# Values of the memory for two heads at once and the Fourier input product in one: 512 moving columns

## The chip, the core and the metric

The kernel runs on one core of a Trainium2 chip. The metric is the device time of one execution in microseconds. Three runs of the kernel before took 1768.17, 1768.70 and 1770.47 us; the median is 1768.7. A profile comes from one more execution.

A core has several engines, each with its own queue of instructions, which it works off strictly in the order in which they stand: TensorE (PE) multiplies matrices, VectorE (DVE) and ScalarE (ACT) work on elements, SyncE (SP) issues the transfers from device memory (DMA), GpSimd (POOL) does next to nothing here. A matmul keeps a 128x128 block stationary in the array and streams the moving operand through it, up to 512 columns; sums gather in accumulators (`acc`), of which the mixing stage has four, each two banks of 512 columns wide.

## The reference, cut to what matters

An encoder of two layers works on two groups of tokens, 512 and 256, with 1024 channels. The even layer mixes by a depthwise convolution of 31 taps (half the channels) and by a Fourier transform along the tokens and inside groups of 128 channels (the other half); the odd layer mixes by average pools of four widths. Each layer then attends with four heads of 256 channels to 256 memory tokens per group, and ends in a gated feed-forward block.

```python
def trunk(...):
    for l in range(DEPTH):
        h = rms_norm(x, norm_mix[l])
        if l % 2 == 0:
            u = h @ w_in_even[e]
            a = conformer_conv(u[..., :D_CONV], u[..., D_CONV:2 * D_CONV], ...)
            f = fourier_mix(u[..., 2 * D_CONV:])
            x = x + jnp.concatenate([a, f], axis=-1) @ w_out_even[e]
        else:
            x = x + multiscale_pool(h, w_pool[o], pool_scale[o])
        x = x + memory_cross_attn(rms_norm(x, norm_xa[l]), rms_norm(mem, norm_mem[l]), ...)
        x = x + swiglu(rms_norm(x, norm_ffn[l]), ...)
...
    kv = (mem_n @ wkv).reshape(b_, m_, 2, XA_HEADS, XA_HEAD_DIM)
    k, v = kv[:, :, 0], kv[:, :, 1]
```

Two products matter here: `u[..., 1024:]`, the Fourier input (768 tokens, 1024 channels in, 512 out), and `v`, the values of the memory (512 memory tokens of both groups, 1024 channels in, 256 out for each head, in both layers).

## The kernel before

**Split numbers.** Every float32 operand of a product is split into an upper and a lower part of a shorter type. `split` (L147, L148) makes the upper part by a copy on ACT (`wh`) and the lower one by a subtraction on DVE (`wl`). A product is the sum of three matmuls, upper x upper, upper x lower, lower x upper, so a block of weights can be used in full only when DVE has made its lower part.

**Weights.** `unit` fetches 128x1024 numbers of weights (512 KB) into one of four buffers `raw` and splits them into two of seven buffers `w`. A buffer is free again when the matmuls that read it are done.

**Even mixer.** `mixer_even` first makes the convolution's two input halves. Each finished chunk of 128 channels adds a generator of taps to a list (`taps`, 46 instructions of 128x392 on DVE at L433 for each of four chunks, each adding to the result of an earlier one); `pump(n)` issues n of them between other work. Then come the Fourier input (`uf`), with the normalized tokens stationary and the weights moving; the transform, four times `along_sequence` and `across_channels`; what is left of keys and values; the sum of the four convolution chunks (`total`, L584 to L586); and the output projection (`project`, `center`).

**Keys and values.** `keys_values` is a generator, which `advance(kv)` moves on by one `yield`. For each head it makes the keys (two units, 24 matmuls of 512 columns each) and the values: both units of weights are fetched and split, and then for each of four blocks of 128 memory tokens 24 matmuls of 256 columns run over the eight blocks of channels into a quarter of one accumulator; when all four are done ACT evicts them (L402). It yields four times for each head. The even mixer advances it once before the transform, twice in it, 12 times in the loop with `pump(8)`, once behind `total`. The odd mixer (`mixer_odd`) advances it twice at its start, once for each of eight pools, and then to the end; behind it come the splits of x for the attention (`split_x`, L150 on ACT, L151 on DVE) and the query product.

**Fourier input.** In two halves of 256 output channels; in each, the token blocks go three to an accumulator, each with 24 matmuls over the eight blocks of channels. ACT and DVE evict the three (L513, L514: a copy and a subtraction, which are the upper and lower part) behind the last of them, with four taps behind each.

**What sets the order.** The program is written as loops, but a scheduler reorders the instructions of each engine by estimated costs and fixes their order when the kernel is built. On the chip nothing moves. It also places the waits: a matmul that writes to an accumulator waits for what reads that accumulator, if that stands ahead of it in the program, whichever of the two banks it reads.

Of the kernel before, what the change touches and what calls it, by code (L numbers as in the profile page):

```python
# [11 lines left out]
F32R = mybir.dt.float32r  # L12
I32 = mybir.dt.int32
AF = mybir.ActivationFunctionType
ALU = mybir.AluOpType
# [50 lines left out]
def trunk_kernel(ctx, tc, x_in, m_in, mt_in, vec_in, cst_in, win, wf, wout, wpool, wq, wk, wv, wo, wgu, wd, out):  # L66
# [35 lines left out]
    def nm(s):  # L102
        cnt[0] += 1
        return f"{s}_{cnt[0]}"
# [25 lines left out]
    def big():  # L130

        return acc.tile([P, 512 * banks], F32, tag="acc", name=nm("acc"))
# [8 lines left out]
    def asf(ap):  # L141
        return ap.bitcast(F32)

    def split(hi, lo, src, gain=None):

        if gain is None:
            nc.scalar.activation(hi, src, AF.Copy)  # L147
            nc.vector.tensor_tensor(lo, src, asf(hi), ALU.subtract)  # L148
        else:
            nc.scalar.activation(hi, src, AF.Copy, scale=gain)  # L150
            nc.vector.scalar_tensor_tensor(lo, src, gain, asf(hi), ALU.mult, ALU.subtract)  # L151
# [26 lines left out]
    def unit(src, n=1024):  # L178

        return parts(fetch(src, n), n)  # L180

    def mm(o, a, b, start, stop, more=False):
        nc.tensor.matmul(o, a, b, start=start, stop=stop, skip_group_check=more)  # L183

    def prod(outs, w, xs, start, stop, more=False):

        wh, wl = w
        for o, (xh, xl) in zip(outs, xs):
            mm(o, wh, xh, start, False, more)
        for o, (xh, xl) in zip(outs, xs):  # L190
            mm(o, wh, xl, False, False, more)
        for o, (xh, xl) in zip(outs, xs):
            mm(o, wl, xh, False, stop, more)

    def cut(p, s):
        return p[0][:, s], p[1][:, s]
# [173 lines left out]
    def keys_values(l, ms, ks, vs):  # L370


        room = stream(512, F32)
        for h in range(HEADS):

            r = [next(room) for _ in range(4)]
            ks.extend([r[0], r[3]])
            ps = big()
            for f in range(2):
                w = unit(wk[l, h * 2 + f])  # L380
                for k in range(KD):
                    prod([ps[:, f * 512 : f * 512 + 512]], cut(w, slice(k * P, (k + 1) * P)), [ms[k]], k == 0, k == KD - 1)
                if f == 0:
                    yield
            for f in range(2):
                nc.scalar.activation(ks[h * 2 + f], ps[:, f * 512 : f * 512 + 512], AF.Copy)
            yield
            w = [unit(wv[l, h, j]) for j in range(2)]
            for r_ in r[1:3]:
                vs.extend([r_[:, :256], r_[:, 256:]])  # L390
            ps = big()
            for t in range(4):
                o = ps[:, t * 256 : (t + 1) * 256]
                for k in range(KD):
                    m_, w_ = cut(ms[k], slice(t * P, (t + 1) * P)), cut(w[k // 4], slice((k % 4) * 256, (k % 4 + 1) * 256))
                    mm(o, m_[0], w_[0], k == 0, False)
                    mm(o, m_[0], w_[1], False, False)
                    mm(o, m_[1], w_[0], False, k == KD - 1)
                if t == 1:
                    yield  # L400
            for t in range(4):
                nc.scalar.activation(vs[h * 4 + t], ps[:, t * 256 : (t + 1) * 256], AF.Copy, scale=mem["r"][:, t : t + 1])  # L402
            yield


    def mixer_even(l, e, first):
# [77 lines left out]
            gated(i, *p)  # L484

        uf = list(zip(blocks(NB, 512), blocks(NB, 512)))
        for j in range(2):
            w = [unit(wf[e, j, 0])]
            if j == 0:
                w.append(unit(wf[e, j, 1]))  # L490
            w = [[cut(u, slice(i * 256, (i + 1) * 256)) for i in range(4)] for u in w]
            if j == 1:
                raw = fetch(wf[e, j, 1])
                hi = wp.tile([P, 1024], F32R, tag="w", name=nm("wh"))
                w.append([])
                for i in range(2):
                    lo, a = hp.tile([P, 512], F32R, tag="h", name=nm("h")), i * 512
                    split(hi[:, a : a + 512], lo, raw[:, a : a + 512])
                    w[1].extend((hi[:, a + b : a + b + 256], lo[:, b : b + 256]) for b in (0, 256))
            for b2 in range(2):  # L500
                ps = big()
                for bb in range(3):
                    b = b2 * 3 + bb
                    o = ps[:, bb * 256 : (bb + 1) * 256]
                    for k in range(KD):
                        x_, w_ = cut(hs[k], slice(b * P, (b + 1) * P)), w[k // 4][k % 4]
                        mm(o, x_[0], w_[0], k == 0, False)
                        mm(o, x_[0], w_[1], False, False)
                        mm(o, x_[1], w_[0], False, k == KD - 1)
                for bb in range(3):  # L510
                    b = b2 * 3 + bb
                    o, u_ = ps[:, bb * 256 : (bb + 1) * 256], cut(uf[b], slice(j * 256, (j + 1) * 256))
                    nc.scalar.activation(u_[0], o, AF.Copy, scale=rt[:, b : b + 1])  # L513
                    nc.vector.scalar_tensor_tensor(u_[1], o, rt[:, b : b + 1], asf(u_[0]), ALU.mult, ALU.subtract)  # L514
                    pump(4)
                if j == 0 and b2 == 0 and "R" not in mem:
                    mem["R"] = stay(token_row(mem["r"], TM), TM, cst, "Rm")

        F = []
        dft = list(zip(blocks(6, 512), blocks(6, 512)))  # L520
# [86 lines left out]
                split(p[0], p[1], xc[i])  # L607
                ln["A"].append(p)

        for _ in range(12):  # L610
            advance(kv)
            pump(8)
        tot = total()
        advance(kv, 1)
        project(1, F, (0,))
# [635 lines left out]
def _arrange(i):  # L1251
    C = np.ascontiguousarray
    k8 = lambda w: w.reshape(KD, P, -1, P).transpose(2, 1, 0, 3)
    d = {}
    d["x"] = _chunks(np.concatenate([i["x_prompt"][0], i["x_sample"][0]], axis=0))
    d["m"] = _chunks(np.concatenate([i["mem_prompt"][0], i["mem_sample"][0]], axis=0))
    d["mt"] = C(np.concatenate([i["mem_prompt"][0], i["mem_sample"][0]], axis=0)).reshape(-1, P, D)
    d["vec"] = C(np.concatenate([
        _cols(i["norm_mix"]), _cols(i["norm_xa"]), _cols(i["norm_mem"]), _cols(i["norm_ffn"]),
        _cols(i["norm_final"][None]), _cols(i["conv_b"]), _cols(i["conv_ln_g"]), _cols(i["conv_ln_b"]),  # L1260
        _cols(i["pool_scale"]),
        i["conv_w"][0].reshape(CW, NC, P).transpose(2, 1, 0).reshape(P, NC * CW),
    ], axis=1))
    d["cst"] = _constants()
    w = i["w_in_even"]
    val = [k8(a[:, :512]) for a in w]
    gate = [k8(a[:, 512:1024]) for a in w]
    d["win"] = C(np.stack([np.stack([g, a], axis=1) for g, a in zip(gate, val)])).reshape(-1, 8, P, 1024)
    d["wf"] = C(w[:, :, 1024:].reshape(-1, 2, 4, P, 2, 256).transpose(0, 4, 1, 3, 2, 5)).reshape(-1, 2, 2, P, 1024)
    d["wout"] = C(i["w_out_even"].reshape(-1, 2, 4, P, 4, 256).transpose(0, 1, 4, 3, 2, 5)).reshape(-1, 2, 4, P, 1024)  # L1270
    d["wpool"] = C(i["w_pool"].reshape(-1, 2, 2, 2, P, 256).transpose(0, 1, 4, 2, 3, 5)).reshape(-1, 2, P, 1024)
    d["wq"] = C(np.stack([k8(a) for a in i["xa_wq"]])).reshape(DEPTH, 8, P, 1024)
    d["wk"] = C(np.stack([k8(a[:, :D]) for a in i["xa_wkv"]])).reshape(DEPTH, 8, P, 1024)
    d["wv"] = C(i["xa_wkv"][:, :, D:].reshape(DEPTH, 2, 4, P, HEADS, 256).transpose(0, 4, 1, 3, 2, 5)).reshape(DEPTH, HEADS, 2, P, 1024)
    d["wo"] = C(i["xa_wo"].reshape(DEPTH, HEADS, 2, P, 2, 512).transpose(0, 1, 4, 3, 2, 5)).reshape(DEPTH, HEADS, 2, P, 1024)
    g = i["ffn_w_gate_up"].reshape(DEPTH, KD, P, 2, NF, P)
    d["wgu"] = C(g.transpose(0, 4, 3, 2, 1, 5)).reshape(DEPTH, NF, 2, P, 1024)
    wd = i["ffn_w_down"].reshape(DEPTH, NPAIR, 2, P, KD // 2, 2, P)
    rows = []
    for l in range(DEPTH):  # L1280

        parts = [wd[l, list(g)].transpose(3, 2, 4, 1, 0, 5).reshape(-1) for g in GROUPS[l]]

        slow = [q for q in range(NPAIR) if not any(q in g for g in GROUPS[l])]
        parts.append(wd[l, slow].transpose(3, 4, 2, 0, 1, 5).reshape(-1))
        rows.append(np.concatenate(parts))
    d["wd"] = C(np.stack(rows))
    return d
# [17 lines left out]
```

## Time and profile before

| | |
|---|---|
| median of three runs | 1768.7 us |
| the profiled execution | 1767.83 us |
| its span, from the first to the last instruction | 1765.7 us |
| TensorE busy | 1745.6 us, 99% |
| DVE busy | 1405.5 us, 80% |
| ACT busy | 762.8 us, 43% |
| matmuls of 128x256 from `wh`, `wl` and `h` | 704 + 328 + 24 |
| mean granted clock of TensorE | 0.997 |

Busy time is counted once where records overlap; a matmul's length is its whole latency, so the step from one start to the next is what it costs TensorE. In rows of the timeline the first number is the start, the second the length, both in us, and `x` the count. In groups the numbers behind the bar are busy time in us, mean length of one in ns, and idle time of the engine just before them with what ended it. Names such as `acc<-wh,s` read result, moving operand, stationary operand.

### The profile page before, as it was taken

Reading aid. Unit: us, or ns where it says so; the run is one execution under the profiler, and the core shown is the slowest. Engines: PE = TensorE matmul, PEld = TensorE weight load, DVE = VectorE, ACT = ScalarE, POOL = GpSimd, SP = SyncE. Lnnn points to the kernel's source line nnn. Section 1 sums busy time; section 2 is a strip of 40 time slices with the busy share of each in tenths; the row PEclk is TensorE's granted clock in tenths of the full one; section 3 lists DMA queues with packets and bytes.
Section 4 is the critical chain, followed back from the end, with each engine's and each line's share of the span. In section 5 each row is a group of like instructions: output and inputs, shape, how many; then the busy total and the mean of one; then the engine's idle time right before and its main releaser. Section 6 shows DMA issues by size and latency. Waiting matters only on the chain.

```text
span 1765.7 us, 26406 instructions
## 1 busy us (share of the span) xinstructions
PE 1745.6 (99%) x10362; PEld 1708.1 (97%) x10362; DVE 1405.5 (80%) x2327; ACT 762.8 (43%) x1287; POOL 2.5 (0%) x40
## 2 busy tenths in 40 slices
PE   9999999999999999999999999999999999999997
PEld 9999999999999999999999999999999999999996
DVE  7998976477788978788769984486888888879876
ACT  7233244253435555454336243352445555543331
POOL 0000000000000000000000000000000000000000
PEclk9999999999999999999999999999999999999998
DMA  7232221202214535456664332111215454547731
GB/s 255 84 108 61 92 77 48 60 22 63 60 48 173 197 135 197 137 181 247 250 234 131 95 96 63 46 48 48 60 36 189 151 189 143 197 171 273 267 86 72
DMA packets 60460, 224.74 MB, mean 127 GB/s; under 512 B 6704, under 2 KB 7984, under 8 KB 60336
## 3 DMA queue, kind: packets, MB, share of 16 engines
q1 hardware_dynamic: 60336, 223.06, 37.4%
q8 instruction: 81, 1.33, 0.3%
q14 instruction: 43, 0.35, 0.1%
HBM read 172.70 MB, written 50.33 MB: 126 GB/s over the span
## 4 chain that ended last, share of the span: by engine, by line
PE 93%; DVE 5%; DMA 1%; ACT 0%; issue 0%; SPq 0%; DVEq 0%; ACTq 0%
PE acc L183 92%; DVE s L151 1%; DVE c L279 1%; DVE s L148 1%; DVE x L323 1%; DVE s L1176 0%; DVE w L148 0%; DMA x<-in_x 0%; PE acc L751 0%; DVE x L816 0%; DMA raw<-in_wd 0%; DVE st L733 0%; DVE c L742 0%; DMA raw<-in_m 0%; DVE kl L148 0%
## 5 line engine op out<-in xcount | busy, mean ns | idle before, releaser
L183 PE MATMUL acc<-s,w 128*128 128x384 f32 x4800 | 835.4, 335 | 0.5 <-DVE x L816 0.4
L183 PEld LDWEIGHTS acc<-s,w 128*128 128x128 f32 x4800 | 831.8, 188 | 2.7 <-issue 0.8
L183 PE MATMUL acc<-s,wh 128*128 128x384 f32 (+2 forms) x2272 | 514.5, 342 | 5.7 <-DVE x L323 2.6
L183 PEld LDWEIGHTS acc<-s,wh 128*128 128x128 f32 x2272 | 403.3, 188 | 20.2 <-ACT Rx L268 3.0
L183 PE MATMUL acc<-s,wl 128*128 128x384 f32 (+2 forms) x1136 | 307.5, 341 | 0.0
L147 ACT ACTIVATE w<-raw 128x512 fp32r<-128x512 f32 (+1 forms) x304 | 181.5, 601 | 255.6 <-PE acc L183 236.0
L148 DVE TENSOR_TENSOR w<-raw,w 128x512 fp32r<-128x512 f32 (+1 forms) x304 | 196.0, 653 | 43.6 <-ACT w L147 39.7
L147 ACT ACTIVATE wh<-raw 128x1024 fp32r<-128x1024 f32 (+2 forms) x107 | 107.3, 1010 | 269.6 <-PE acc L183 252.2
L183 PEld LDWEIGHTS acc<-s,wl 128*128 128x128 f32 x1136 | 206.3, 188 | 5.3
L148 DVE TENSOR_TENSOR wl<-raw,wh 128x1024 fp32r<-128x1024 f32 (+2 forms) x105 | 122.4, 1173 | 77.7 <-PE acc L183 64.2
L183 PE MATMUL acc<-wh,s 128*128 128x256 f32 x704 | 129.0, 284 | 0.0
L816 DVE TENSOR_TENSOR x<-acc,x 128x384 f32<-128x384 f32 x168 | 92.6, 554 | 24.9 <-PE acc L183 24.2
L183 PEld LDWEIGHTS acc<-wh,s 128*128 128x128 f32 x704 | 110.7, 192 | 0.2
L323 DVE TENSOR_TENSOR x<-acc,x 128x768 f32<-128x768 f32 x80 | 76.2, 955 | 30.1 <-PE acc L183 30.0
L147 ACT ACTIVATE w<-sum 128x512 fp32r<-128x512 f32 (+1 forms) x120 | 71.9, 599 | 60.5 <-PE acc L183 42.5
L148 DVE TENSOR_TENSOR w<-sum,w 128x512 fp32r<-128x512 f32 (+1 forms) x120 | 78.4, 653 | 24.0 <-ACT w L147 23.5
L183 PE MATMUL acc<-wl,s 128*128 128x256 f32 x328 | 92.9, 283 | 0.0
L183 PE MATMUL acc<-s,s 128*128 128x512 f32 (+3 forms) x456 | 80.6, 335 | 0.0
L183 PEld LDWEIGHTS acc<-s,s 128*128 128x128 f32 x456 | 70.3, 190 | 9.5 <-issue 0.5
L433 DVE SCALAR_TENSOR_TENSOR c<-c,vec,c 128x392 f32<-128x392 f32 x124 | 70.3, 627 | 0.2
L816 DVE TENSOR_TENSOR pair<-acc,c 128x384 f32<-128x384 f32 x72 | 40.0, 556 | 32.7 <-ACT c L1048 21.0
L183 PEld LDWEIGHTS acc<-wl,s 128*128 128x128 f32 x328 | 63.0, 192 | 0.2
(146 smaller groups left out, 1541.1 us busy)
## 6 DMA issues: line engine op xcount, KB each, us to landing
raw<-in_wgu SPq DMA_DIRECT2D x88, 512.0 KB, 3.7
pk<-s SPq DMA_DIRECT2D x52, 768.0 KB, 4.1
s<-pk SPq DMA_DIRECT2D x52, 768.0 KB, 6.8
raw<-in_wd SPq DMA_DIRECT2D x32, 384.0 KB, 3.2
raw<-in_wk SPq DMA_DIRECT2D x16, 512.0 KB, 3.7
raw<-in_wv SPq DMA_DIRECT2D x16, 512.0 KB, 3.7
raw<-in_wq SPq DMA_DIRECT2D x16, 512.0 KB, 3.7
raw<-in_wo SPq DMA_DIRECT2D x16, 512.0 KB, 3.6
```

Source lines behind the costliest of these rows:

```text
L147: nc.scalar.activation(hi, src, AF.Copy)
L148: nc.vector.tensor_tensor(lo, src, asf(hi), ALU.subtract)
L151: nc.vector.scalar_tensor_tensor(lo, src, gain, asf(hi), ALU.mult, ALU.subtract)
L183: nc.tensor.matmul(o, a, b, start=start, stop=stop, skip_group_check=more)
L279: nc.vector.tensor_tensor(s, s, q, ALU.add)
L323: nc.vector.tensor_tensor(two(x[d]), halves(ps), two(x[d]), ALU.add)
L433: nc.vector.scalar_tensor_tensor(out_, src[:, a : a + CL], w, prev, ALU.mult, ALU.add)
L816: add = lambda o, a, b: nc.vector.tensor_tensor(o, a, b, ALU.add)
```

## The change

The values are made for two heads together. The weights of a unit now are two blocks of channels for 512 output columns (two heads), four units for a pair of heads. The loop over units stands outside, that over the four blocks of memory tokens inside, so that two accumulators are in use from the first unit to the last, and each matmul has 512 moving columns. The keys of both heads are made before. There are six `yield`s for a pair of heads. The Fourier input is made likewise: four units, inside them all six blocks of tokens, three accumulators in use throughout. With the last unit each block is evicted as soon as its own matmuls stand, in the inner loop. The evictions cover 512 columns. Taps come two by two behind each of 24 block steps; the loop behind the transform has eight rounds with `pump(12)`. The weights lie in device memory in the new order.

```diff
+        for h in range(0, HEADS, 2):
+            r = [next(room) for _ in range(8)]
+            for i in range(2):
...
+            own = [r[2], r[5], r[6], r[7]]
+            vs.extend(own[t][:, i * 256 : (i + 1) * 256] for i in range(2) for t in range(4))
+            ps = [big() for _ in range(2)]
+            for u in range(4):
+                w = unit(wv[l, h // 2, u])
+                for t in range(4):
+                    o = ps[t // 2][:, (t % 2) * 512 : (t % 2 + 1) * 512]
+                    for i in range(2):
+                        k = u * 2 + i
+                        m_, w_ = cut(ms[k], slice(t * P, (t + 1) * P)), cut(w, slice(i * 512, (i + 1) * 512))
+                        mm(o, m_[0], w_[0], k == 0, False)
+                        mm(o, m_[0], w_[1], False, False)
+                        mm(o, m_[1], w_[0], False, k == KD - 1)
+                    if u == 3:
+                        nc.scalar.activation(own[t], o, AF.Copy, scale=mem["r"][:, t : t + 1])
+                if u % 2:
                     yield
...
-        for j in range(2):
-            w = [unit(wf[e, j, 0])]
...
+        ps = [big() for _ in range(3)]
+        for u in range(4):
+            w = unit(wf[e, u])
+            for b in range(NB):
+                o = ps[b // 2][:, (b % 2) * 512 : (b % 2 + 1) * 512]
                 for i in range(2):
...
+                    k = u * 2 + i
+                    x_, w_ = cut(hs[k], slice(b * P, (b + 1) * P)), cut(w, slice(i * 512, (i + 1) * 512))
+                    mm(o, x_[0], w_[0], k == 0, False)
+                    mm(o, x_[0], w_[1], False, False)
+                    mm(o, x_[1], w_[0], False, k == KD - 1)
+                if u == 3:
+                    nc.scalar.activation(uf[b][0], o, AF.Copy, scale=rt[:, b : b + 1])
+                    nc.vector.scalar_tensor_tensor(uf[b][1], o, rt[:, b : b + 1], asf(uf[b][0]), ALU.mult, ALU.subtract)
+                pump(2)
+            if u == 0 and "R" not in mem:
+                mem["R"] = stay(token_row(mem["r"], TM), TM, cst, "Rm")
...
-        for _ in range(12):
+        for _ in range(8):
             advance(kv)
-            pump(8)
+            pump(12)
```

The order of the built programs differs at three places that matter below. Line numbers of the changed kernel are 13 lower or 1 higher there: its taps are L434, its convolution sums L571 to L573, its Fourier evictions L501.

**First place**, DVE, end of the convolution taps in the even mixer. `c_2020` and `c_1680` are the fourth chunk's result, `wl_2120` is the last lower part for the values of the fourth head, `wl_2255` that of the first output projection. Before:

```order
L148 TENSOR_TENSOR wl_2074<-raw_2071,wh_2073 128x1024
L433 SCALAR_TENSOR_TENSOR c_2020<-c_2019,vec,c_2020 128x392
L148 TENSOR_TENSOR wl_2114<-raw_2111,wh_2113 128x1024
L433 SCALAR_TENSOR_TENSOR c_2020<-c_2019,vec,c_2020 128x392 x8
L148 TENSOR_TENSOR wl_2120<-raw_2117,wh_2119 128x1024
L433 SCALAR_TENSOR_TENSOR c_2020<-c_2019,vec,c_2020 128x392 x18
L148 TENSOR_TENSOR wl_2255<-raw_2252,wh_2254 128x1024
```

Now, where `wl_1739`, `wl_1769`, `wl_1831` and `wl_1861` are the lower parts of the four units for the values of the third and fourth head, and `wl_1895` that of the first output projection:

```order
L148 TENSOR_TENSOR wl_1739<-raw_1736,wh_1738 128x1024
L434 SCALAR_TENSOR_TENSOR c_1680<-c_787,csum,c_1680 128x392
L148 TENSOR_TENSOR wl_1769<-raw_1766,wh_1768 128x1024
L434 SCALAR_TENSOR_TENSOR c_1680<-c_787,csum,c_1680 128x392
L571 TENSOR_TENSOR c_1824<-c_390,c_900 128x784
L434 SCALAR_TENSOR_TENSOR c_1680<-c_1679,vec,c_1680 128x392
L572 TENSOR_TENSOR c_1824<-c_1824,c_1468 128x784
L434 SCALAR_TENSOR_TENSOR c_1680<-c_1679,vec,c_1680 128x392 x30
L148 TENSOR_TENSOR wl_1831<-raw_1828,wh_1830 128x1024
L573 TENSOR_TENSOR c_1824<-c_1824,c_1680 128x784
L148 TENSOR_TENSOR wl_1861<-raw_1858,wh_1860 128x1024
L148 TENSOR_TENSOR wl_1895<-raw_1892,wh_1894 128x1024
```

The lower parts of the last two value units stand behind a block of 30 taps; before, both of the last head's stood ahead of the block of 18.

**Second place**, the end of the Fourier input, now. On TensorE, `acc_798`, `acc_799` and `acc_800` hold two token blocks each; these are the matmuls of the last unit (`wh_976`, `wl_977`) with the last block of channels but one and the last (`s_168`, `s_171`):

```order
L183 MATMUL acc_799<-wh_976,s_171 128x512
L183 MATMUL acc_800<-wh_976,s_168 128x512
L183 MATMUL acc_800<-wl_977,s_168 128x512
L183 MATMUL acc_798<-wh_976,s_168 128x512
L183 MATMUL acc_798<-wl_977,s_168 128x512
L183 MATMUL acc_798<-wh_976,s_168 128x512
```

Ahead of the first of these rows stand the last unit's six matmuls of the first and five of the third token block; the fourth row is the first of the second token block, which shares `acc_798` with the first. On DVE, before that accumulator's first eviction (`s_796<-acc_798`):

```order
L148 TENSOR_TENSOR wl_923<-raw_920,wh_922 128x1024
L434 SCALAR_TENSOR_TENSOR c_900<-c_455,csum,c_900 128x392
L148 TENSOR_TENSOR wl_977<-raw_974,wh_976 128x1024
L434 SCALAR_TENSOR_TENSOR c_900<-c_455,csum,c_900 128x392 x9
L148 TENSOR_TENSOR wl_1069<-raw_1066,wh_1068 128x1024
L434 SCALAR_TENSOR_TENSOR c_900<-c_455,csum,c_900 128x392
L434 SCALAR_TENSOR_TENSOR c_900<-c_899,vec,c_900 128x392 x12
L148 TENSOR_TENSOR wl_1143<-raw_1140,wh_1142 128x1024
L434 SCALAR_TENSOR_TENSOR c_900<-c_899,vec,c_900 128x392 x2
L501 SCALAR_TENSOR_TENSOR s_796<-acc_798,rt_302,s_794 128x512
```

Before, the evictions stood behind all of an accumulator's matmuls, and the next ones went to another accumulator.

**Third place**, ACT, end of the odd mixer. L402 evicts values, L150 makes the upper part of x for the attention. Before:

```order
L386 ACTIVATE s_10011<-acc_10012 128x512
L150 ACTIVATE s_10188<-x_101,vec 128x768
L150 ACTIVATE s_10191<-x_102,vec 128x768
...
L150 ACTIVATE s_10206<-x_107,vec 128x768
L147 ACTIVATE wh_10275<-raw_10273 128x1024
L147 ACTIVATE wh_10374<-raw_10372 128x1024
L402 ACTIVATE s_10010<-acc_10087,rm 128x256 x4
```

Now:

```order
L147 ACTIVATE wh_9814<-raw_9812 128x1024
L402 ACTIVATE s_9275<-acc_9502,rm 128x512
L402 ACTIVATE s_9276<-acc_9502,rm 128x512
L402 ACTIVATE s_9276<-acc_9503,rm 128x512
L402 ACTIVATE s_9277<-acc_9503,rm 128x512
L150 ACTIVATE s_9628<-x_101,vec 128x768
L150 ACTIVATE s_9631<-x_102,vec 128x768
```

The seven splits for the attention have moved from ahead of the last evictions of values to behind them.

More of the change, by code (lines that the diff above doesn't have):

```diff
@@ L373, in keys_values @@
         room = stream(512, F32)
[L374 to L383, printed above, removed]
-                    yield
[L385 to L403, printed above, removed]
@@ new lines, in keys_values @@
+        for h in range(0, HEADS, 2):
+            r = [next(room) for _ in range(8)]
+            for i in range(2):
+                ks.extend([r[i * 3], r[i * 3 + 1]])
+                ps = big()
+                for f in range(2):
+                    w = unit(wk[l, (h + i) * 2 + f])
+                    for k in range(KD):
+                        prod([ps[:, f * 512 : f * 512 + 512]], cut(w, slice(k * P, (k + 1) * P)), [ms[k]], k == 0, k == KD - 1)
+                    if f == 0:
+                        yield
+                for f in range(2):
+                    nc.scalar.activation(ks[(h + i) * 2 + f], ps[:, f * 512 : f * 512 + 512], AF.Copy)
+                yield
+            own = [r[2], r[5], r[6], r[7]]
[14 more added lines that the diff above has]
+                if u % 2:
+                    yield
@@ L486, in mixer_even @@
         uf = list(zip(blocks(NB, 512), blocks(NB, 512)))
-        for j in range(2):
-            w = [unit(wf[e, j, 0])]
[L489 to L495, printed above, removed]
-                for i in range(2):
[L497 to L517, printed above, removed]
@@ L1268, in _arrange @@
     d["win"] = C(np.stack([np.stack([g, a], axis=1) for g, a in zip(gate, val)])).reshape(-1, 8, P, 1024)
-    d["wf"] = C(w[:, :, 1024:].reshape(-1, 2, 4, P, 2, 256).transpose(0, 4, 1, 3, 2, 5)).reshape(-1, 2, 2, P, 1024)
+    d["wf"] = C(w[:, :, 1024:].reshape(-1, 4, 2, P, 512).transpose(0, 1, 3, 2, 4)).reshape(-1, 4, P, 1024)
     d["wout"] = C(i["w_out_even"].reshape(-1, 2, 4, P, 4, 256).transpose(0, 1, 4, 3, 2, 5)).reshape(-1, 2, 4, P, 1024)
@@ L1273, in _arrange @@
     d["wk"] = C(np.stack([k8(a[:, :D]) for a in i["xa_wkv"]])).reshape(DEPTH, 8, P, 1024)
-    d["wv"] = C(i["xa_wkv"][:, :, D:].reshape(DEPTH, 2, 4, P, HEADS, 256).transpose(0, 4, 1, 3, 2, 5)).reshape(DEPTH, HEADS, 2, P, 1024)
+    d["wv"] = C(i["xa_wkv"][:, :, D:].reshape(DEPTH, 4, 2, P, HEADS // 2, 512).transpose(0, 4, 1, 3, 2, 5)).reshape(DEPTH, HEADS // 2, 4, P, 1024)
     d["wo"] = C(i["xa_wo"].reshape(DEPTH, HEADS, 2, P, 2, 512).transpose(0, 1, 4, 3, 2, 5)).reshape(DEPTH, HEADS, 2, P, 1024)
```

## The prediction

> **What bounds the kernel now.** I read the page first (span, busy shares, the chain that ended last), then the waits of TensorE, then stretches of the timelines around the two products that change.
>
> ```profile
> span 1765.7 us, 26406 instructions
> PE 1745.6 (99%) x10362; PEld 1708.1 (97%) x10362; DVE 1405.5 (80%) x2327; ACT 762.8 (43%) x1287; POOL 2.5 (0%) x40
> PE 93%; DVE 5%; DMA 1%; ACT 0%; issue 0%; SPq 0%; DVEq 0%; ACTq 0%
> ...
> PE acc L183 <- DVE c L250: 4.8, 2, 3.7
> PE acc L183 <- DVE x L323: 2.6, 2, 1.4
> ```
>
> TensorE is busy for 99% of the span and 93% of the chain, so a matmul that is saved is time saved, and a wait of TensorE that is added is time lost, one for one. Its listed waits are few and small; the answer for waits between 50 and 300 us and between 1000 and 1090 us, the two mixers, is empty. What the average hides is the second engine: in the even mixer VectorE (DVE) is full. From 149.15 to 219.24 us it never waits:
>
> ```profile
> 149.15 0.17 DVE L553 COPY c<-c 128x2 f32<-128x2 f32 x1 [3.42 <-ACT c L547]
> ...
> 219.24 0.99 DVE L586 TENSOR_TENSOR c<-c,c 128x784 f32<-128x784 f32 x1
> ...
> L433 DVE SCALAR_TENSOR_TENSOR c<-c,vec,c 128x392 f32<-128x392 f32 x62 | 34.6, 631 | 0.0
> L433 DVE SCALAR_TENSOR_TENSOR c<-c,csum,c 128x392 f32<-128x392 f32 x30 | 17.1, 625 | 0.0
> L148 DVE TENSOR_TENSOR wl<-raw,wh 128x1024 fp32r<-128x1024 f32 x12 | 14.7, 1226 | 0.0
> L709 DVE TENSOR_TENSOR s<-s,Rm 128x512 f32<-128x512 f32 x2 | 1.4, 700 | 0.0
> ```
>
> The groups are those of that stretch: 92 convolution taps (L433) and 12 weight splits (L148). TensorE waits for none of it now, because each split is done some microseconds before its weights are used. That is the cover that the change touches.
>
> **What it removes: narrow matmuls.** 768 value products (2 layers, 4 heads, 96 each) and 288 Fourier products of 256 columns become 384 and 144 of 512. Both shapes run now, so both prices are rows (start, duration, count):
>
> ```profile
> 87.46 0.40 PE L183 MATMUL acc<-wh,s 128*128 128x256 f32 x2
> ...
> 113.02 0.28 PE L183 MATMUL acc<-wh,s 128*128 128x256 f32 x1
> 113.14 0.40 PE L183 MATMUL acc<-s,wh 128*128 128x512 f32 x1
> ...
> 199.81 0.63 PE L183 MATMUL acc<-s,wh 128*128 128x512 f32 x2
> ...
> 210.72 0.28 PE L183 MATMUL acc<-wh,s 128*128 128x256 f32 x1
> ```
>
> From 87.46 to 113.02 lie 213 steps of the narrow kind: 0.1200 us each. From 199.81 to 210.72 lie 48 of the wide kind: 0.2273 us. One wide for two narrow saves 12.7 ns, and 528 of them save **6.7 us**; bounds 6.6 and 7.0 (0.2267 us, the step in the middle of a run). The Trainium skill, "TensorE: Matmul & The Clock Gate", section "Back-to-back issue gap", gives 262 and 518 cycles at 2.4 GHz for the two widths; by it a pair would save 2.5 ns and all of them 1.3 us, and the sum below would end 5.4 us later. The rows have both shapes in this kernel and decide against it.
>
> The loads stay 20 units of 512 KB, 16 for the values and 4 for the Fourier product. They land in 3.7 us, and four buffers let them run ahead:
>
> ```profile
> raw<-in_wv SPq DMA_DIRECT2D x16, 512.0 KB, 3.7
> ```
>
> I cost them at nothing; without that lead a unit would cost its 3.7 us. Evictions get fewer and wider, off the path except where named below.
>
> **What it adds: four waits of TensorE.** The order of the changed program is fixed per engine, so each wait is one sum for the engine that is waited for against one for TensorE.
>
> *Weights of the second value pass, even layer.* Let t0 be the end of the last Fourier product on TensorE (149.17 us now, where DVE starts its full stretch).
>
> ```profile
> 147.82 1.51 PE L183 MATMUL acc<-s,s 128*128 128x258 f32 x12
> 149.17 0.33 PE L183 MATMUL acc<-wh,s 128*128 128x256 f32 x1
> ...
> 160.84 1.22 DVE L148 TENSOR_TENSOR wl<-raw,wh 128x1024 fp32r<-128x1024 f32 x1
> 161.97 4.93 DVE L433 SCALAR_TENSOR_TENSOR c<-c,csum,c 128x392 f32<-128x392 f32 x9
> ```
>
> In the new order TensorE does 24 + 96 + 96 + 48 wide matmuls from t0, then two with the upper part of the third value unit, and needs its lower part wl_1831: 266 x 0.2273 = t0 + 60.5 us. DVE has that split behind one block of 30 taps (first place in the order rows). Up to its end it holds the same 92 taps and the first two sums, 9 splits where the old stretch has 12, and neither of the two L709. A split takes 1.13 us (160.84 to 161.97), an L709 0.60 (0.70 less 0.1 of overlap). So 70.1 - 3 x 1.13 - 2 x 0.60 = 65.5, and 0.1 for the end of the last: t0 + 65.6. TensorE waits **5.1 us**. What stands behind it is late together with it, the fourth unit's split follows 2 us later and is then in time. Bounds: 4.0 if the tap blocks run without any gap, 6.2 if the start of DVE slips by 1 us.
>
> *Fourier product, last weight block.* Two token blocks share an accumulator, and the second one's last six matmuls now wait until DVE has read the first (second place). Prices:
>
> ```profile
> 77.74 0.28 PE L183 MATMUL acc<-wh,s 128*128 128x256 f32 x1
> ...
> 86.37 1.02 PE L183 MATMUL acc<-c,ones 128*128 128x256 f32 x4
> 87.04 0.47 PE L183 MATMUL acc<-wh,s 128*128 128x256 f32 x1
> 87.35 0.28 PE L183 MATMUL acc<-wl,s 128*128 128x256 f32 x1
> ...
> 87.92 1.23 DVE L148 TENSOR_TENSOR wl<-raw,wh 128x1024 fp32r<-128x1024 f32 x1
> ...
> 92.09 5.26 DVE L433 SCALAR_TENSOR_TENSOR c<-c,csum,c 128x392 f32<-128x392 f32 x8
> ...
> L151 DVE SCALAR_TENSOR_TENSOR s<-raw,vec,s 128x512 fp32r<-128x512 f32 x16 | 11.9, 749 | 0.2
> ```
>
> TensorE starts the stage at 77.74 as now, pays 0.86 for the row of ones (86.37 to 87.35, less one step) and reaches the waiting matmul after 122 wide ones: 77.74 + 0.86 + 27.7 = 106.3. DVE comes to its split of 87.92 with unchanged work; behind it stand three more splits, 25 taps and the eviction. Eight taps took 5.26 at 92.09, 0.66 a step where each waits for its own predecessor; nine took 4.93 at 161.97, 0.54. Eleven at the first and 14 at the second price are 14.8, four splits 4.5, the eviction 0.75 as the 512-wide sibling: 108.0. Wait **1.8 us**; all taps at 0.54 make it 0.4, all at 0.66 3.4.
>
> *End of the odd mixer.* There the last value pass has nothing to mix in (third place). The fourth block of tokens waits for ScalarE to evict the third from the same accumulator, and the query product of the attention waits for seven splits that now stand behind the last eviction.
>
> ```profile
> 1064.00 5.89 ACT L150 ACTIVATE s<-x,vec 128x768 fp32r<-128x768 f32 x7
> ...
> 1074.35 0.86 PE L183 MATMUL acc<-s,wh 128*128 128x384 f32 x4
> ...
> L150 ACT ACTIVATE s<-x,vec 128x768 fp32r<-128x768 f32 x46 | 41.5, 933 | 27.4 <-DVE x L323 22.4 <-DMA x<-in_x 2.7 <-DVE x L816 2.2
> L402 ACT ACTIVATE s<-acc,rm 128x256 f32<-128x256 f32 x32 | 12.5, 475 | 2.5 <-PE acc L183 2.4
> L386 ACT ACTIVATE s<-acc 128x512 f32<-128x512 f32 x16 | 8.7, 594 | 26.5 <-PE acc L183 26.5
> L268 ACT ACTIVATE Rx<-acc 128x768 f32<-128x768 f32 x4 | 3.2, 811 | 2.0 <-PE acc L183 2.0
> ```
>
> Now those seven start at 1064, ten microseconds ahead of the query product at 1074.35. A scaled eviction of 512 columns I take at 0.69: 0.475 for 256 and 256 more at 0.85 ns, the step from 0.594 for 512 to 0.811 for 768. The third block's last matmul starts two steps after the second's; counted from the latter, 0.39 until it ends (a wide matmul's length) and two evictions in a row, 0.1 overlapped, are 1.67, while TensorE could go on after three steps, 0.68: **1.0 us**. After the fourth block 0.39, one eviction (0.69) and one split (0.93) come before the next matmul, which could start after 0.23: **1.8 us**. Bounds together 1.5 and 3.3; nothing in the program's order lies there that could hide them.
>
> *The clock.* A wait of 5.1 us is longer than any in this trace outside the last stage, and there the granted clock (the column after the POOL's) did this:
>
> ```profile
> 1744.00:1747.50 3.50, 2.35 (x17) 1.90 (x17) 2.94 (x7) 1.14 (x3) 0.00 (x0) 1.00 0.01 2
> 1747.50:1750.90 3.40, 3.40 (x28) 3.16 (x27) 2.77 (x5) 0.42 (x1) 0.00 (x0) 1.00 0.00 0
> 1750.90:1754.30 3.40, 2.65 (x21) 2.31 (x19) 3.36 (x8) 0.83 (x2) 0.00 (x0) 1.00 0.61 231
> 1754.30:1757.80 3.50, 0.00 (x0) 0.00 (x0) 3.13 (x13) 0.00 (x0) 0.00 (x0) 0.51 0.77 294
> ```
>
> After 3.4 us of thin work it was halved. A hole of 5.1 us should halve it too. No row shows the way back; if it takes a stretch as long as the way down, 3.4 us at half speed do the work of 1.7, so I take **1.7 us** (an estimate from these rows), bounds 0 and two stretches, 3.4. The same page of the Trainium skill, "Part 1: The HAM clock gate", says that one idle window of 3.4 us throttles and about as long at work releases; the fall agrees with the row, the release is shown by no run here.
>
> Sum: -6.7 + 5.1 + 1.8 + 1.0 + 1.8 + 1.7 = **+4.7 us**. The profiled execution took 1767.8 us, 0.9 under the median of the three runs, 1768.7; on the median, **1773.4 us**.
>
> **Rivals.** (a) *The hole does not halve the clock*, or it is back at once: 1768.7 + 3.0 = 1771.7. For it: the whole span up to 1754 us ran at full clock; against it: no wait there was longer than 1.4 us. (b) *Costlier*: the clock falls at the Fourier wait and at the end of the odd mixer as well, some 1.7 each, 1776.8. For it: those holes fill half a stretch of 3.4; against it: the stretch at 1744 with a third of it empty kept its clock. (c) *Not slower*: DVE is not behind at the two splits and evictions, so that only the shorter matmuls count: 1768.7 - 6.7 = 1762.0. It needs DVE to reach wl_1831 five microseconds sooner, by t0 + 60; from waits under 3.2 us in all it would be faster by more than can be told. For it: the empty list of waits now, in the same stages; against it: the 65.5 us are this trace's own, and nothing in the order lets DVE overtake its taps. That the change would not widen its matmuls is excluded by the order.
>
> **How the numbers follow.** Forecast 0.52, (a) 0.23, (b) 0.17, (c) 0.08. Between 1765.2 and 1772.2 (0.2% around the median, what a measurement of this kernel can tell from no change) fall (a), a part of the forecast where one wait is smaller, and little of (c): same 0.30, faster 0.07, slower 0.63. The range runs from 1769.5, (a) with two waits at their lower bounds, to 1777.0, (b); the forecast's own is 1771.5 to 1775.5.
>
> **What would show it.** In the profile after: 128x256 groups with wh and wl gone and 528 more of 128x512 near 0.227 us a step; a wait of PE on a weight split (wl, L148) of about 5 us near 210 us, the largest of the span, and the granted clock under 1.00 right behind it; about 2 us on DVE's Fourier eviction (L501) near 106; two waits on ACT, 1 and 1.8 us, near 1070 to 1080. DVE without idle time between the last Fourier product and that split. Wrong would be the theory if the wait near 210 is under 3 us or its releaser is a DMA or ACT, and wrong the gain if the wide value products step at more than 0.235 us.

## The result: 0.6% slower, more than twice as much as forecast

| | before | changed |
|---|---|---|
| median of nine executions of the changed kernel, in two sessions | | 1779.96 us (1775.01 to 1783.28) |
| medians of the kernel before in the same two sessions | 1768.43 and 1768.19 us | |
| ratio in the first session, 95% interval | | 1.0058 (1.0036 to 1.0080) |
| ratio in the second | | 1.0068 (1.0056 to 1.0081) |
| span of the profiled execution | 1765.7 us | 1779.5 us |

The forecast was 1773.4 us with a range from 1769.5 to 1777.0. The direction was right, the size was not: 11.5 us were lost instead of 4.7, and the time lies outside the range.

The page of the changed kernel answers the first lines quoted of before (93% of the chain on TensorE there):

```profile
span 1779.5 us, 25322 instructions
PE 1749.5 (98%) x9834; PEld 1687.4 (95%) x9834; DVE 1406.2 (79%) x2320; ACT 760.1 (43%) x1264; POOL 2.5 (0%) x40
PE 84%; DVE 13%; DMA 1%; ACT 1%; issue 1%; SPq 0%; DVEq 0%; ACTq 0%
...
L183 PE MATMUL acc<-wh,s 128*128 128x512 f32 x352 | 113.7, 398 | 2.1 <-DVE s L501 1.2
...
L183 PE MATMUL acc<-wl,s 128*128 128x512 f32 x176 | 70.0, 398 | 4.9 <-DVE wl L148 4.9
```

The narrow groups with weights are gone, there are 528 matmuls fewer (9834 instead of 10362), and DVE's share of the chain rose from 5 to 13%. Although TensorE has less to do, its busy time rose, from 1745.6 to 1749.5 us. That is the first sign of a lower clock. The waits of TensorE from 50 to 1300 us (total, times, longest):

```profile
PE acc L183 <- DVE wl L148: 4.9, 1, 4.9
PE acc L183 <- DVE c L279: 3.4, 2, 1.7
PE acc L183 <- ACT Rx L268: 1.8, 2, 0.9
PE acc L183 <- ACT s L150: 1.6, 1, 1.6
PE acc L183 <- DVE s L501: 1.2, 1, 1.2
...
PE acc L183 <- ACT s L402: 0.9, 1, 0.9
```

Four of them were forecast, at these places and on these releasers: the weight split (L148), the Fourier eviction (L501), the value eviction (L402), the attention's split (L150). The wait on L268 stands in the kernel before too. The one on L279, the sum of squares at the start of the feed-forward stages, was not forecast. In the timeline:

```profile
106.16 0.39 PE L183 MATMUL acc<-wl,s 128*128 128x512 f32 x1
107.71 0.50 PE L183 MATMUL acc<-wh,s 128*128 128x512 f32 x1 [1.16 <-DVE s L501]
...
208.74 0.84 PE L183 MATMUL acc<-wh,s 128*128 128x512 f32 x3
214.44 0.79 PE L183 MATMUL acc<-wl,s 128*128 128x512 f32 x1 [4.87 <-DVE wl L148]
...
483.41 0.51 PE L183 MATMUL acc<-s,wl 128*128 128x384 f32 x2
485.61 2.08 PE L183 MATMUL acc<-ones,c 128*128 128x1 f32 x12 [1.69 <-DVE c L279]
...
1007.50 0.39 PE L183 MATMUL acc<-wh,s 128*128 128x512 f32 x1
...
1018.42 1.75 PE L183 MATMUL acc<-s,w 128*128 128x384 f32 x9
...
1080.33 0.39 PE L183 MATMUL acc<-wh,s 128*128 128x512 f32 x1
1081.62 0.50 PE L183 MATMUL acc<-wh,s 128*128 128x512 f32 x1 [0.91 <-ACT s L402]
...
1082.89 0.39 PE L183 MATMUL acc<-wh,s 128*128 128x512 f32 x1
1084.88 0.97 PE L183 MATMUL acc<-s,wh 128*128 128x384 f32 x4 [1.60 <-ACT s L150]
```

DVE is where the prediction put it, with the late split behind one block of 30 taps and not a moment idle:

```profile
196.16 0.96 DVE L572 TENSOR_TENSOR c<-c,c 128x784 f32<-128x784 f32 x1
197.04 16.21 DVE L434 SCALAR_TENSOR_TENSOR c<-c,vec,c 128x392 f32<-128x392 f32 x30
213.17 1.22 DVE L148 TENSOR_TENSOR wl<-raw,wh 128x1024 fp32r<-128x1024 f32 x1
```

The gain first: 48 wide steps from 1007.50 to 1018.42 are 0.2275 us each. In other passes of the same kernel they are up to 0.2285, and the narrow ones of before were 0.1199 to 0.1200, so a pair saves 11 to 12.5 ns, all 528 about 6.3 us (forecast 6.7). A hole is a stretch in which TensorE starts nothing. Counted from step to step, the four are 1.3, 5.0, 1.1 and 1.8 us, 9.2 together (forecast 1.8 + 5.1 + 1.0 + 1.8 = 9.7).

What was missed is the clock. These stretches of 4 us of the changed kernel show its four falls (places where the granted clock drops to a half); the granted clock is the column behind POOL's:

```profile
209.00:213.00 4.00, 0.58 (x3) 0.15 (x1) 4.00 (x8) 1.06 (x1) 0.00 (x0) 1.00 0.00 0
213.00:217.00 4.00, 2.56 (x6) 2.07 (x7) 4.00 (x5) 0.00 (x0) 0.00 (x0) 0.53 0.37 111
217.00:221.00 4.00, 4.00 (x12) 3.11 (x12) 4.00 (x7) 0.00 (x0) 0.00 (x0) 0.61 0.78 241
...
482.00:486.00 4.00, 2.31 (x16) 1.99 (x14) 3.90 (x5) 1.43 (x2) 0.00 (x0) 1.00 0.68 182
486.00:490.00 4.00, 4.00 (x18) 4.00 (x19) 2.62 (x12) 0.00 (x0) 0.00 (x0) 0.54 0.67 214
490.00:494.00 4.00, 4.00 (x16) 4.00 (x15) 0.70 (x1) 0.00 (x0) 0.00 (x0) 0.60 0.00 1
...
1086.00:1090.00 4.00, 4.00 (x20) 4.00 (x20) 4.00 (x5) 4.00 (x6) 0.00 (x0) 0.64 0.28 112
...
1274.00:1278.00 4.00, 4.00 (x19) 4.00 (x19) 3.11 (x12) 0.00 (x0) 0.00 (x0) 0.60 0.67 217
```

In the trace the clock is at a half for 6.8, 6.8, 3.4 and 3.4 us. Each step there, less the step of the same shape at full clock, adds up to 2.7, 3.3, 1.7 and 1.7 us, together 9.3 with rounding. The kernel before has no such stretch between its first 7 and its last 12 us. The balance of the two spans is -6.3 + 9.2 + 9.3 = +12.2, and 13.8 was measured; of the rest 0.6 is a wait on L803 near 943 us, 0.2 the waits of the feed-forward stages, and 0.8 lies in delays under 0.3 us that are not placed.

Two of the four falls lie at 486 and 1275 us, in the feed-forward stages, where the change edits nothing. Before, the same work stood there like this:

```profile
469.63 0.34 PE L183 MATMUL acc<-s,wh 128*128 128x384 f32 x1
471.15 0.80 PE L183 MATMUL acc<-s,wh 128*128 128x384 f32 x3 [1.18 <-DVE x L323]
...
479.07 0.51 PE L183 MATMUL acc<-s,wl 128*128 128x384 f32 x2
479.82 1.50 PE L183 MATMUL acc<-ones,c 128*128 128x1 f32 x12 [0.23 <-DVE c L279]
```

DVE is late by nearly the same in both kernels: the waits of TensorE for it come to 1.7 to 1.8 us in each stage before and to 1.9 now. Before, they stood in two pieces: for an accumulator that DVE's last residual (L323) still read, and ahead of the twelve thin 128x1 products (in layer 1 nearly all of it, 1.6 us, in the first). In the changed kernel the first wait is gone, because the accumulators come round in another order (the run `fill_hole` below bears on this), and all of it stands in one piece, with 1.5 us of thin products directly behind. The sum of the waits hardly changes, from 3.5 to 3.7 us in both layers; their grouping does.

### The profile page after: what moved, and what is told of

Read it like the earlier page. It is cut to its first block, busy times and chain, and to the rows that moved or that the text cites. A ratio compares the mean times of both kernels' runs of the same rounds, so it can differ in the third digit from the quotient of the medians.

```text
span 1779.5 us, 25322 instructions
## 1 busy us (share of the span) xinstructions
PE 1749.5 (98%) x9834; PEld 1687.4 (95%) x9834; DVE 1406.2 (79%) x2320; ACT 760.1 (43%) x1264; POOL 2.5 (0%) x40
## 4 chain that ended last, share of the span: by engine, by line
PE 84%; DVE 13%; DMA 1%; ACT 1%; issue 1%; SPq 0%; DVEq 0%; ACTq 0%
PE acc L183 83%; DVE c L434 5%; DVE s L151 1%; DVE wl L148 1%; DVE c L279 1%; DVE s L148 1%; DMA raw<-in_m 1%; DVE x L323 1%; DMA raw<-in_wd 0%; DVE s L1163 0%; ACT s L150 0%; DMA x<-in_x 0%; PE acc L738 0%; DVE c L461 0%; DVE w L148 0%
## 5 line engine op out<-in xcount | busy, mean ns | idle before, releaser
L148 DVE TENSOR_TENSOR w<-raw,w 128x512 fp32r<-128x512 f32 (+1 forms) x304 | 195.4, 650 | 43.4 <-ACT w L147 39.0
L148 DVE TENSOR_TENSOR wl<-raw,wh 128x1024 fp32r<-128x1024 f32 (+2 forms) x106 | 123.4, 1169 | 98.5 <-PE acc L183 81.6
L803 DVE TENSOR_TENSOR x<-acc,x 128x384 f32<-128x384 f32 x168 | 92.4, 553 | 29.8 <-PE acc L183 29.4
L183 PE MATMUL acc<-wh,s 128*128 128x512 f32 x352 | 113.7, 398 | 2.1 <-DVE s L501 1.2
L323 DVE TENSOR_TENSOR x<-acc,x 128x768 f32<-128x768 f32 x80 | 76.1, 953 | 30.4 <-PE acc L183 30.4
L148 DVE TENSOR_TENSOR w<-sum,w 128x512 fp32r<-128x512 f32 (+1 forms) x120 | 78.0, 650 | 24.8 <-ACT w L147 24.1
L183 PEld LDWEIGHTS acc<-wh,s 128*128 128x128 f32 x352 | 67.4, 191 | 19.0 <-ACT s L402 3.3
L183 PE MATMUL acc<-wl,s 128*128 128x512 f32 x176 | 70.0, 398 | 4.9 <-DVE wl L148 4.9
L434 DVE SCALAR_TENSOR_TENSOR c<-c,vec,c 128x392 f32<-128x392 f32 x124 | 69.6, 617 | 0.3
L803 DVE TENSOR_TENSOR pair<-acc,c 128x384 f32<-128x384 f32 x72 | 39.9, 554 | 33.9 <-ACT c L1035 21.5
L151 DVE SCALAR_TENSOR_TENSOR s<-x,vec,s 128x768 fp32r<-128x768 f32 x46 | 45.5, 1011 | 12.8 <-ACT s L150 12.8
```

The source lines that it names most:

```text
L323: nc.vector.tensor_tensor(two(x[d]), halves(ps), two(x[d]), ALU.add)
L434: nc.vector.scalar_tensor_tensor(out_, src[:, a : a + CL], w, prev, ALU.mult, ALU.add)
L803: add = lambda o, a, b: nc.vector.tensor_tensor(o, a, b, ALU.add)
```

## The experiments

The theory after the two traces: holes as forecast, and a clock that falls at each place where a long hole, or a hole and thin work together, leaves TensorE with little to do. Its rival: that the falls are only a by-product, and the time is lost in the wide matmuls or in DVE.

### Each half of the change alone

`values_only` has the new `keys_values`, with its loop of eight rounds, and the old Fourier block; `fourier_only` the reverse. Here and below the edits are shortened.

```diff
-            w = unit(wf[e, u])          # values_only: the Fourier block of before
+            w = [unit(wf[e, j, 0])]
...
-        for h in range(0, HEADS, 2):    # fourier_only: the values of before
+        for h in range(HEADS):
```

> Only the values of the memory are made for two heads at once; the Fourier input product is the old one. Against before: 384 pairs x 12.7 ns = -4.9 us, the wait for wl of the second value pass +4.9, the end of the odd mixer +2.5 (its two waits for ACT, 0.9 and 1.6). Theory (the granted clock falls to a half wherever a hole of TensorE is long enough or is followed by thin matmuls): a fall behind the 4.9 us hole (2.7), one at the end of the odd mixer (1.6) and one in the feed-forward stage of layer 1, where the order has one hole of 1.9 us directly before the 128x1 products (1.6); none in the feed-forward stage of layer 0, where the same wait stands in two pieces as in before (1.35 and 0.3). 1768.4 + 2.5 + 5.9 = 1776.8 (1775 to 1778.5). Rival (one fall, as predicted): 1768.4 + 2.5 + 1.7 = 1772.6.

> Only the Fourier input product is made with 512 columns; the values are the old ones. Against before: 144 pairs x 12.7 ns = -1.8 us, the wait of the last weight block +1.4. Theory (grouped holes let the clock fall): in layer 0's feed-forward stage the order has one hole of 1.9 us directly before the 128x1 products, so a fall there (1.6 to 2.7), in layer 1's it has two pieces and no fall: 1769.7 to 1770.7. Rival (the feed-forward stages have no part in it): 1768.0, granted clock 1.00 there.

Values alone took 1778.27 us, ratio 1.0050 (1.0036 to 1.0064): theory. The profile has falls behind the weight split's wait and in layer 1's feed-forward stage, and none in layer 0's, where the waits stand in two pieces. The fall at the end of the odd mixer did not come in that execution. (This profile and that of `splits_first_odd` have one more fall of 3.4 us near 12 us, at the start of the kernel, which the change does not touch.) Fourier alone took 1769.48 us, ratio 1.0006 (0.9997 to 1.0015), between the two forecasts and not to be told from no change. Its profile is instructive: the hole in layer 0 is there in one piece, and the clock did not fall.

```profile
478.00:482.00 4.00, 2.30 (x18) 1.98 (x17) 3.37 (x7) 1.06 (x1) 0.00 (x0) 1.00 0.69 216
482.00:486.00 4.00, 4.00 (x25) 4.00 (x24) 2.29 (x9) 0.00 (x0) 0.00 (x0) 1.00 0.46 131
```

So this hole does not let the clock fall in every execution; `splits_first_odd` and `three_cures` below each have one such hole without a fall too. The eleven executions of this kernel lie between 1767.71 and 1771.42 us.

### The changed kernel once more

> The changed kernel once more, to see how far its executions differ. Theory (the number of falls of the clock varies, since the windows of about 3.4 us in which the throttle decides do not start with the kernel): 1775 to 1781.5, and the mean granted clock of an execution, 0.992 to 0.995, follows its time at about 1.8 us for each 0.001. Rival (the spread is something else): no relation of clock and time.

Time and mean granted clock of all nine executions of the changed kernel:

| mean granted clock | times, us |
|---|---|
| 0.995 | 1775.01 |
| 0.994 | 1778.02, 1778.53 |
| 0.993 | 1779.96 |
| 0.992 | 1779.94, 1781.27, 1781.32, 1781.76 |
| 0.991 | 1783.28 |

The time follows the clock, by about 2 us for each 0.001. In the profile of this run the falls are at 214 (3.4 us), 487 (3.4) and 1269 us (6.8), and the one at the end of the odd mixer is missing: same program, same holes, other falls. The last section shows what differs.

### Work in the holes

Two kernels put needless matmuls where TensorE stands idle. They leave DVE as late as it was. `fill_ffn` ran beside the changed kernel; the runs behind it are of two later sessions, in each of which the kernel before took 1767.99 us instead of 1768.19.

```diff
         ps = big()
+        for _ in range(8):              # fill_ffn, token_root in the feed-forward stages
+            mm(ps[:, 128:512], dummy[:, :P], dummy[:, :H], True, True)
...
                 w = unit(wv[l, h // 2, u])
+                if l == 0 and h == 2 and u == 2:     # fill_hole
+                    d = big()
+                    for _ in range(20):
+                        mm(d[:, :512], ms[4][0][:, :P], w[0][:, :512], True, True)
```

> The changed kernel with eight needless matmuls of 384 columns ahead of the 128x1 products in both feed-forward stages (1.4 us of work each, into columns of the accumulator that nobody reads). Theory (the clock falls because TensorE stands idle 1.9 us and then has only thin products): the hole shrinks from 1.9 to 0.5 us, no fall of the granted clock in either stage, and the time is 2.7 + 1.6 = 4.3 us shorter although TensorE does more: 1779.9 - 4.3 = 1775.6. Rival (the half clock is no cost of its own, or comes from the thin products alone): falls stay at these places and the time stays at 1779.9.

> The changed kernel with twenty needless matmuls of 512 columns at the hole of the even mixer (20 x 0.227 = 4.55 us of work ahead of the wait for wl of the third value unit, into an accumulator that nobody reads). The wait itself is not removed: 4.55 us of work and some 0.4 of waiting take the place of 5.0 of waiting. Theory (half of what the wait costs more than its length is the clock behind it): no fall of the granted clock between 205 and 230 us, 1.6 to 2.7 us shorter than the changed kernel, 1779.9 - 2.2 = 1777.7. Rival (the fall costs nothing, or comes anyway): 1779.9, clock 0.7 or less in the stretch behind.

`fill_ffn` took 1777.67 us, 2.3 less than the changed kernel beside it (1779.96), with 1.4 us of work more in each stage. The intervals of the two ratios to the kernel before overlap (1.0050, 1.0037 to 1.0062, and 1.0068, 1.0056 to 1.0081), so the time alone does not show this gain. Expected were 4.3; the forecast took the falls of one execution for those of all. Its profile has no fall in either stage:

```profile
482.00:486.00 4.00, 3.69 (x24) 3.37 (x22) 3.90 (x5) 1.18 (x2) 0.00 (x0) 1.00 0.75 221
486.00:490.00 4.00, 4.00 (x27) 4.00 (x27) 3.07 (x12) 0.00 (x0) 0.00 (x0) 1.00 0.58 175
490.00:494.00 4.00, 4.00 (x25) 4.00 (x24) 0.00 (x0) 0.00 (x0) 0.00 (x0) 1.00 0.00 1
```

The thin products are still there, only the hole ahead of them is filled. In the feed-forward stages of these profiles the fall came only where both stood together. `fill_hole` took 1775.09 us, 4.9 less than the changed kernel, where 2.2 were expected. In the place itself it did what was expected:

```profile
209.00:213.00 4.00, 4.00 (x19) 3.33 (x18) 4.00 (x9) 1.06 (x1) 0.00 (x0) 1.00 0.00 0
213.00:217.00 4.00, 3.70 (x16) 2.74 (x15) 4.00 (x6) 0.00 (x0) 0.00 (x0) 1.00 0.17 39
217.00:221.00 4.00, 4.00 (x19) 3.31 (x18) 4.00 (x7) 0.61 (x1) 0.00 (x0) 1.00 0.85 280
```

DVE reaches the split no sooner, TensorE does 4.5 us of needless work, and yet the kernel is faster: the clock stays, and one part of the gain was not planned. The edit takes one accumulator more, and with that the waits in layer 0's feed-forward stage fall apart again:

```profile
PE acc L183 <- DVE c L279: 1.7, 1, 1.7
...
PE acc L183 <- DVE x L323: 1.4, 1, 1.4
```

Only layer 1 still has its one hole (L279, once instead of twice), and only there the clock falls. This is also the evidence for the cause of the grouping in layer 0: it hangs on the place in the rotation of accumulators. In the traces TensorE, DVE and ACT do the same instructions in the same order around the thin products in the kernel before, the changed one, both halves and this one, so the accumulators are what is left to differ. For layer 1, where `values_only` regrouped the wait and `fourier_only` did not, there is no such test.

### Each wait taken away

```diff
-        for _ in range(8):              # no_wait_even
+        for _ in range(9):
             advance(kv)
-            pump(12)
+            pump(11)
         tot = total()
-        advance(kv, 1)
...
-        advance(kv, 16)                 # splits_first_odd: end of mixer_odd
+        (attention, behind its split_x:)
+            advance(rest, 16)
```

> The changed kernel with nine instead of eight rounds of the loop behind the transform, 11 taps in each, and without the last step of the values behind the convolution sums: the splits of the last two value units stand among the taps, not behind all of them. Theory: the wait of 5.0 us and the fall behind it go, and nothing takes their place, since the convolution sums are not needed until two output projections later: 1779.9 - 5.0 - 2.2 = 1772.7. Rival (DVE is simply full: what is late is late, and the wait turns up at the sum of the convolution instead): a new wait of 2 to 5 us on DVE between 215 and 245 us, 1776 to 1779.

> The changed kernel with the splits of x for the attention of layer 1 written ahead of the last value pass of the odd mixer, not behind it. Theory: ScalarE makes the seven splits ten microseconds earlier, as in the kernel before, the waits at 1075 to 1085 us (0.9 for the third block's eviction, 1.8 for the split) go or shrink to under 1 us together, and the clock no longer falls behind them, where it did in some executions: 1779.9 - 2.3 - 1.0 = 1776.6. Rival (the evictions of the values are then late, behind splits that wait for x): a wait on the evictions of 1 to 3 us in the same place, 1779 to 1780.

Without the late step of the values the kernel took 1773.49 us, 6.5 less than the changed kernel's 1779.96 (7.2 expected), and TensorE waits nowhere from 110 to 300 us. DVE's work is the same and nothing else is late: the 5 us were not a lack of DVE time but a matter of order. A loop of eight steps with 12 taps, and then one whole step behind all remaining taps, had put two weight splits behind 30 taps. With the splits of x written first, 1774.65 us were measured, 5.3 less (3.3 expected); both waits on ACT at the end of the odd mixer and the fall behind them are gone:

```profile
1078.00:1082.00 4.00, 4.00 (x23) 3.58 (x22) 1.25 (x2) 2.26 (x5) 0.00 (x0) 1.00 0.01 4
1082.00:1086.00 4.00, 4.00 (x25) 4.00 (x24) 0.00 (x0) 0.32 (x1) 0.00 (x0) 1.00 0.42 131
```

I had taken 0.9 + 1.8 less a small rest; the whole 2.9 went. The clock's part cannot be split off more exactly than the falls vary.

### All cures together, and their controls

`all_cures` adds to these two the evictions in pairs and the 128x1 products inside the second plain product. `three_cures` leaves the last one out; `before_late_root` is the kernel before with the last one alone.

```diff
-                if u == 3:
+                if u == 3 and b % 2:    # both blocks of an accumulator, then both evictions; values likewise
+                    for c in (b - 1, b):
...
-        r = token_root(square_sum(x), T, 1.0 / D, RMS_EPS)
-        p0 = pg, plain(0, 1)
+        sq, root = square_sum(x), []
+        p0 = pg, plain(0, 1, lambda: root.append(token_root(sq, T, 1.0 / D, RMS_EPS)), 3)
+        r = root[0]
```

> The changed kernel with all of it: values finished among the taps, splits of x ahead of the last value pass, evictions of values and of the Fourier input only when both blocks of an accumulator are done, and in both feed-forward stages the 128x1 products inside the second plain product instead of ahead of it. Wide matmuls as in the changed kernel. Theory: what is left is the gain of the wide matmuls (6.1 to 6.7) and the two holes of 1.9 us that the kernel before has in its feed-forward stages too: 1768.2 - 6.4 - 3.7 = 1758.1, no fall of the clock before the last stage. Rival (TensorE's time is given back elsewhere, the cures collide): 1764 to 1768, a new wait of more than 1 us in one of the three places.

> As the run with all cures, but the feed-forward stages left as they are in the changed kernel. Theory (what the change costs is all in its own three places and in the clock): the two holes of 1.9 us ahead of the 128x1 products come back (+3.7) and with them a fall of the clock at each in most executions (0 to 2.7 each, 1.7 on average): 1757.9 + 3.7 + 3.0 = 1764.6, holes 3.7 in all and the half clock only behind them. Rival (the cure in the feed-forward stages brought nothing): 1758.

> The kernel before with only the cure in the feed-forward stages: the 128x1 products inside the second plain product. Theory (the wide matmuls, and not this, make the run with all cures fast): there the waits for the last residual's accumulator, 1.35 in layer 0 and 1.6 in layer 1, are not touched by it, only the 0.5 ahead of the 128x1 products: 1768.2 - 0.6 = 1767.6. Rival (the ten microseconds come from the feed-forward stages): 1758 to 1764.

| | median, us | ratio to before, 95% interval |
|---|---|---|
| all cures | 1757.92 | 0.9945 (0.9933 to 0.9958) |
| three cures | 1764.35 | 0.9977 (0.9968 to 0.9986) |
| before, late root | 1766.89 | 0.9996 (0.9987 to 1.0005) |

All three came out within 0.7 us of the theory. The kernel with all cures is 10 us faster than the one before, at a mean granted clock of 0.997. Its page and all its waits of TensorE from 50 to 1300 us:

```profile
span 1756.0 us, 25317 instructions
...
PE 94%; DVE 3%; DMA 1%; ACT 0%; issue 0%; SPq 0%; DVEq 0%; ACTq 0%
```

```profile
PE acc L183 <- ACT Rx L268: 1.8, 2, 0.9
PE acc L183 <- DVE x L806: 0.9, 3, 0.4
PE acc L183 <- DVE s L148: 0.4, 2, 0.2
PE acc L183 <- DVE c L279: 0.2, 1, 0.2
```

The late root alone is worth nothing that can be measured in the kernel before, because there the waits for the accumulator (1.35 and 1.6) stay. Behind the other three cures it removes both holes of 1.9 us and the falls behind them, and is worth 6.4 us (1764.35 to 1757.92). The kernel with all cures and `before_late_root` differ by 9.0 us, of which those waits are 3.0, so some 6 us are the wide matmuls: the gain of the change was there all the time, under its waits. That the wide matmuls themselves bring the clock down is excluded: this kernel has all 528 of them and no fall ahead of the last stage.

## Why the prediction was wrong, point by point

- **What bounds the kernel:** right. TensorE sets the end, and DVE without idle time in the even mixer is what the change ran into.
- **Gain of the wide matmuls, 6.7:** 6.3 by the steps, about 6 by the run with all cures. The cycles that the Trainium skill, "TensorE: Matmul & The Clock Gate", section "Back-to-back issue gap", gives for isolated matmuls, by which it would have been 1.3, are not borne out in these dense passes.
- **Wait for the weight split, 5.1:** 4.87 in the row, 5.0 by steps. The sum of 92 taps, nine splits and two sums held, and the clock fell behind it.
- **Fourier eviction, 1.8:** 1.3, inside its bounds of 0.4 and 3.4. (The terms written down, 108.0 less 106.3, give 1.7.)
- **End of the odd mixer, 1.0 and 1.8:** 1.1 and 1.8.
- **The clock, 1.7:** this is the step that failed. The sum held one fall of one stretch; the profiled execution has four falls, which cost 9.3 us. (The median execution is 1.4 us shorter, so there it may be some 8.) Three things were wrong. First, the price: a fall lasts one or two stretches of 3.4 us, and in these profiles one cost 1.5 to 1.7 us and two 2.4 to 3.3; the price of two stood among the bounds and was not carried into the range for more than one place. Second, the places: the end of the odd mixer was named, but in a rival only, and the feed-forward stages were not looked at, because the change has no line there. The wait on L323 was quoted from the page of before (2.6, two times), but not whether it stays where it is in the changed program; only the waits that the edit adds were followed. Third, the condition: the prediction asked how long a hole is, and the traces go by how little of a stretch of 3.4 us is filled, with thin products not counted (last section).
- **The rivals:** (b), costlier falls, had the right mechanism at too few places: it added the Fourier wait, where none of seven profiles shows a fall, and the odd mixer, where three of six do.
- **The reading of the last stage,** where a stretch with a third of it empty kept its clock, was right for the Fourier hole and misled for holes with thin work behind them: the busy column counts a 128x1 product in full.

## What to carry to other kernels

Price a hole of the bounding engine with the clock behind it, thin products beside it counted as part of the hole, and look for it in all stages: a reordered pool of buffers can push two small waits into one without changing their sum. Where an edit shortens one engine's work, list which steps of the program now stand whole behind another engine's long block; moving one step by one loop round was worth 6.5 us here. A spread of the times that follows the mean granted clock is a hint that holes are near the point of a fall, and filling or splitting a hole then pays even if the wait stays.

## What was unexpected of the hardware

In the profiles of these runs, between the first 7 us and the last stage, the half clock lasts 3.4 or 6.8 us and nothing between, and ends by itself under full work. The hole of 5.0 us brought it in five of five profiles, the hole of 1.9 us with 1.5 us of thin products behind it in ten of thirteen, the two holes at the end of the odd mixer (1.1 and 1.8, followed by the thin products of the attention) in three of six. Holes of 1.35 to 1.6 us with full work behind them brought it in none of seven, nor did the Fourier hole in seven, nor a hole of 0.5 us ahead of the thin products in two. The Trainium skill, "TensorE: Matmul & The Clock Gate", "Part 1: The HAM clock gate", says that the throttle decides by windows of 3413 ns that run free of the kernel; the lengths and the change from execution to execution agree with that. The Trainium skill, "TensorE: Matmul & The Clock Gate", section "HAM oscillation — how this bites in real kernels", warns of idle gaps of over about 3.4 us; that is too mild here: gaps of 1.9 us were enough with thin work behind.

How little work is too little can be counted in the traces. From its first rise on, every change of the clock lies on a grid of 3.413 us; in the changed kernel the four falls come 61, 141, 317 and 372 steps behind the rise. Take for each step the share in which matmuls stream: each from its start for 0.444 ns a column (the 0.2275 us for 512), at most to the next start, and a 128x1 product as nothing. Between 50 and 1725 us the twelve profiles have 5857 steps that begin at full clock. The 18 emptiest, with shares from 0 to 0.39, are those with a fall at their end, and there is no other fall; the next, at 0.40, kept the clock. A half clock went on for a second step where the first, counted at half speed, was filled to 0.77 or less (ten falls), and ended where it was 0.83 or more (ten, the two near 12 us among them). That is why the same hole brings a fall in one execution and not in the next: it matters how the grid lies across the hole and the thin products behind it. The count is of these kernels' shapes only, and how it carries to others stays open.
